# Hyena filters split into two parts where they are made, stored in both parts, and loaded so for the sums over n1

## The chip, the cores and the metric

The kernel runs on one core of one Trainium2 chip. The metric is the device time of one execution in microseconds. TensorE's clock has two levels, 2.4 and 1.2 GHz; the profile prints the granted clock as a share of the higher one.

## The reference, cut to what matters

One encoder block on x of 2048 x 1024, float32: a projection, differential attention, a Hyena mixer, a merge, and a mixture of 16 experts. The part that matters here is the Hyena mixer with its implicit filters:

```
filt = (hid @ w_out).reshape(l, HYENA_ORDER, 2, HYENA_WIDTH)      # hid: 2048 x 64
filt = filt * exp(-t[:, None] * deltas[None, :])[:, None, None, :]
kern = concatenate([filt[:, :, 0], zeros(1, ...), filt[:0:-1, :, 1]])
spec = rfft(kern, axis=0)
...
hy = short_conv(u @ w_in[hyena columns])       # width 3; z, g1, g2 of 512 channels each
for n in range(2):
    z = gates[n] * (long_conv(z, spec[:, n]) + skip[n] * z)
```

So there are 2 orders x 2 sides x 512 channels of filters of 2048 taps, and each is brought into the frequency domain once.

## The kernel before

float32 products are made on TensorE from two parts: a number a is written as a high part (a rounded copy, type F32R) and a low part (a minus the high part), and `mm3` does three matmuls, high x high, low x high and high x low. `split` makes the parts with a copy on ScalarE and a subtraction on VectorE, `split_pool` with the subtraction on POOL instead.

Every engine takes its instructions in order. The order is set when the program is built: a list scheduler goes through the instructions as written and places each by its own estimate of when it can start; pools with a fixed number of buffers make it wait for the last reader of a buffer. DMAs are issued by SP (`nc.sync`), ScalarE (`nc.scalar`) and POOL (`nc.gpsimd`), each in its own order.

**Making the filters** (`filter_gen`, called from `proj_phase` as `gen`, 309 to 600 us). The projection of the Hyena columns goes through column blocks 3, 4 and 5 of 512 columns (`weights(3 + c)`), each of 8 row blocks: a load "r" of 256 KB on SP (four buffers) and its split into "wh" and "wl" (nine buffers each). A column block has 4 x 4 groups of 24 matmuls (tile "p", operands "uh", "ul" and "wh", "wl"). Beside it, `filter_gen` is a generator whose 64 pieces are spread over the first 46 of these 48 groups. It goes through 4 channel tiles (ct), 2 orders (o), 4 stretches of 512 taps (i) and 2 combinations of the two sides (s). For each ct and o it loads and splits a factor ("wo", "weo", "woh", "wol"); for each i it loads the decay ("dc", SP) and the hidden rows ("hs", POOL); for each s two matmuls write "fq", VectorE multiplies it by the decay into "fo" (ring of two), and `store_l1` stores "fo" in two DMAs on SP of 128 KB, in rows of 512 bytes.

**Using them** (`hyena_phase`, 1510 to 2100 us). The length is split in two factors, and the transform is a sum over n1 (`first`), a middle transform (`spectrum` or `conv`) and, for the way back, a sum over the second factor (`last`, which loads "vr" on SP, splits it into "vh" and "vl", and whose matmuls are "p<-vh,d"). There are 12 `first`s: 8 of filters, 4 of the signal. Each takes 8 tiles of four channels from the generator `parts_of`: a load "zr" of 256 KB on SP (ring of three), then `split_pool` into "zh" (ScalarE) and "zl" (POOL). For each tile there are 4 x 3 matmuls of 256 columns ("p<-d,zh" and "p<-d,zl"), and the result is split into "bh" (ScalarE) and "bl" (VectorE), two of each a tile. The tails of the convolution before (tables "tg" on POOL, "yl" on POOL, "vo" on ScalarE, stored as s_v on ScalarE's queue) and `last` run beside a `first`, as does the making of the gates (loads "gu" on POOL) beside the first two.

Of the kernel before, what the change touches and what calls it, by code (L numbers as in the profile page):

```python
# [9 lines left out]
F32 = mybir.dt.float32  # L10
F32R = mybir.dt.float32r
# [8 lines left out]
L = 2048  # L20
# [73 lines left out]
def proj_phase(E, x, norm1_g, w_in, conv_w, conv_b, qg, kg, rope, qn, kn, vs, hyc, ud, sg, mlp, gen):  # L94
# [6 lines left out]
    with ExitStack() as ctx:  # L101
# [76 lines left out]
        with pool_of(tc, name="pj_q", bufs=2) as pq:  # L178
            with pool_of(tc, name="pj_x", bufs=4) as px, pool_of(tc, name="pj_pt", bufs=3, space=PSUM) as pt:
                turn(0, px, pt)  # L180
                w = weights(0)
                gq = pc.tile([128, 2, DK], F32, name="gq")
                nc.sync.dma_start(gq[:, 0], dap(qg, 0, [[0, 128], [1, DK]]))
                nc.sync.dma_start(gq[:, 1], dap(kg, 0, [[0, 128], [1, DK]]))
                rp = pc.tile([128, NT, 2, 16], F32, name="rp")
# [443 lines left out]
def filter_gen(E, w, tabs, hsd, filt):  # L629

    nc, tc = E.nc, E.tc
    with pool_of(tc, name="fl_o", bufs=2, side="right") as po, pool_of(tc, name="fg_ps", bufs=2, space=PSUM) as ps:
        for ct in range(4):
            for o in range(2):
                wo = po.tile([128, 2, 128], F32, name="wo", bufs=1)
                for s in range(2):
                    nc.sync.dma_start(wo[s * 64:(s + 1) * 64], w["w_out"][0].rearrange("h (o s c) -> h o s c", o=2, s=2)
                                      [:, o, :, ct * 128:(ct + 1) * 128])
                weo = po.tile([128, 2, 128], F32, name="weo", bufs=1)
                nc.vector.tensor_tensor(weo[:, 0], wo[:, 0], wo[:, 1], ALU.add)  # L640
                nc.vector.tensor_tensor(weo[:, 1], wo[:, 0], wo[:, 1], ALU.subtract)
                wh = po.tile([128, 2, 128], F32R, name="woh")
                wl = po.tile([128, 2, 128], F32R, name="wol")
                split(nc, wh, wl, weo)
                for i in range(4):
                    dc = po.tile([128, 512], F32, name="dc")
                    nc.sync.dma_start(dc, tabs["decay"][ct * 128:(ct + 1) * 128, i * 512:(i + 1) * 512])
                    hs = po.tile([128, 512], F32R, name="hs")
                    nc.gpsimd.dma_start(hs, hsd[:, i * 512:(i + 1) * 512])
                    fs = []  # L650
                    for s in range(2):
                        p = ps.tile([128, 512], F32, name="fq")
                        for a, ww in enumerate((wh, wl)):
                            nc.tensor.matmul(p, ww[:, s], hs, start=a == 0, stop=a == 1)
# [5 lines left out]
                    if i == 0:  # L660
                        c = po.tile([128, 1], F32, name="c0")
                        nc.vector.tensor_tensor(c, fs[0][:, 0:1], fs[1][:, 0:1], ALU.add)
                        nc.vector.tensor_scalar(fs[0][:, 0:1], c, 0.5, None, ALU.mult)
                    for s in range(2):
                        store_l1(nc.sync, filt, (o * 2 + s) * CW * L, ct, i, fs[s])
                    yield


def hyena_phase(E, hyc, filt, skip, tabs, scr, hT, filler, then):
# [7 lines left out]
    with pool_of(tc, name="hy_d", bufs=1) as pd, ExitStack() as right:  # L677
        with ExitStack() as ctx:
# [21 lines left out]
            with pool_of(tc, name="hy_e", bufs=1) as pe:  # L700
                ex = pe.tile([8, 128], F32, name="ex")
                nc.sync.dma_start(ex, tabs["ex"])
                sk = pe.tile([8, 2, 64], F32, name="sk")
                for o in range(2):
                    nc.sync.dma_start(sk[:, o], dap(skip, o * CW, [[64, 8], [1, 64]]))
                skb = pd.tile([128, 2, 64], F32, name="skb")
                p = s1.tile([128, 128], F32, name="p1")
                nc.tensor.matmul(p, ex, sk.rearrange("p o g -> p (o g)"), start=True, stop=True)
                nc.scalar.activation(skb, p.rearrange("p (o g) -> p o g", o=2), AF.Copy)
# [13 lines left out]
            def parts_of(jobs):  # L723

                todo = [(src, hf * 8 + q) for src, hf in jobs for q in range(8)]
                loads, ready = [], []

                def load():
                    src, q = todo.pop(0)
                    r = p1.tile([128, 4, 128], F32, name="zr", bufs=AHEAD)  # L730
                    nc.sync.dma_start(r, dap(src, q * 512, [[8192, 128], [128, 4], [1, 128]]))
                    loads.append(r)

                def cut():
                    r = loads.pop(0)
                    zh = p1.tile([128, 4, 128], F32R, name="zh", bufs=CUT[0])
                    zl = p1.tile([128, 4, 128], F32R, name="zl", bufs=CUT[0])
                    split_pool(zh, zl, r)
                    ready.append((zh, zl))
                    if todo:  # L740
                        load()
# [3 lines left out]
                cut()  # L745
                while ready:
                    while loads and len(ready) < CUT[0]:
                        cut()
                    yield ready.pop(0)

            AHEAD, CUT = 3, [2]

            def first(it, v, side, busy=False):
# [3 lines left out]
                for q in range(8):  # L757
                    zh, zl = next(it)
# [980 lines left out]
```

## Time and profile before

| | us |
|---|---|
| median of 3 runs (3725.71 to 3728.37) | 3728.32 |
| the profiled execution | 3731.11 |
| its span | 3729.3 |
| making the filters beside the projection | 309 to 600 |
| attention | 690 to 1510 |
| the twelve sums over n1, with all between | 1533 to 2035 |

The profile is of one execution; its engines' times are read against its own span. A window gives the busy time of each engine in a stretch, and TensorE's granted clock. A timeline gives each instruction's start, and the idle time ahead of it with what ended it. A tile's answer gives the durations of all instructions that read or write it, and of its DMAs the time from issue to landing.

### The profile page before, as it was taken

What the parts mean: (1) busy time and instruction counts of PE and PEld (TensorE: products, weight loads), DVE (VectorE), ACT (ScalarE), POOL (GpSimd) and SP (SyncE); (2) the same over time, 40 slices, a digit from 0 to 9 for tenths busy, and PEclk for the clock granted to TensorE, in tenths of its full rate; (3) what the DMA queues carried; (4) which work ended last, traced back from release to release, by engine and by line L of the source; (5) the groups of instructions that cost most, each with busy time, mean ns of one, the idle gap of its engine ahead of it and who ended that gap; (6) DMA issues with size and microseconds to landing.
All of it is one profiled execution on the core that took longest, in us unless ns stands there. A gap on an engine that the chain in (4) does not pass through costs nothing. (4 is left out here: it accounts for less than half of the span.)

```text
span 3729.3 us, 55700 instructions
## 1 busy us (share of the span) xinstructions
PE 3608.1 (97%) x21122; PEld 3117.1 (84%) x21122; DVE 2472.5 (66%) x5459; ACT 1819.2 (49%) x2787; POOL 412.9 (11%) x423
## 2 busy tenths in 40 slices
PE   8999999999999999999999799998999999999998
PEld 6788888788888888788998678887998888888887
DVE  8944552598989898256787754548875666665663
ACT  5411111566676666357667533323445555555553
POOL 0000000000000000344553200000000101101000
PEclk9999999999999999999999899998999999999999
DMA  4286774322222231757776853324666766766664
GB/s 157 75 246 170 193 187 135 119 64 68 96 81 94 68 102 60 227 165 227 210 214 192 286 170 130 115 91 138 216 194 204 222 206 208 221 203 210 220 204 123
DMA packets 449713, 607.28 MB, mean 163 GB/s; under 512 B 37467, under 2 KB 333411, under 8 KB 442789
## 3 DMA queue, kind: packets, MB, share of 16 engines
q1 hardware_dynamic: 388149, 436.71, 37.1%
q0 software_dynamic: 34736, 127.16, 12.7%
q10 hardware_dynamic: 26560, 39.85, 3.0%
q8 instruction: 166, 2.72, 0.3%
q14 instruction: 102, 0.84, 0.1%
HBM read 464.16 MB, written 139.46 MB: 162 GB/s over the span
## 5 line engine op out<-in xcount | busy, mean ns | idle before, releaser
L43 DVE TENSOR_TENSOR wl<-r,wh 128x2048 fp32r<-128x2048 f32 (+1 forms) x248 | 476.9, 1928 | 333.1 <-ACT wh L42 333.0
L42 ACT ACTIVATE wh<-r 128x2048 fp32r<-128x2048 f32 (+1 forms) x248 | 402.5, 1624 | 383.6 <-PE pg L1616 138.4
L1616 PE MATMUL pg<-x,wh 128*128 128x512 f32 x1664 | 587.0, 398 | 0.0
L1619 PE MATMUL pg<-x,wl 128*128 128x256 f32 x1664 | 466.3, 280 | 0.0
L1616 PEld LDWEIGHTS pg<-x,wh 128*128 128x128 f32 x1664 | 312.4, 188 | 75.3
L411 DVE TENSOR_SCALAR_CACHE_REDUCE x<-p 128x512 f32<-128x512 f32 x512 | 335.0, 685 | 22.8 <-PE p L410 22.0
L410 PE MATMUL p<-k,qT 128*128 128x512 f32 x1024 | 327.3, 415 | 0.0
L1619 PEld LDWEIGHTS pg<-x,wl 128*128 128x128 f32 x1664 | 314.1, 189 | 0.5
L418 ACT ACTIVATE x<-x,sm 128x2048 f32<-128x2048 f32 x128 | 256.7, 2005 | 45.8 <-DVE sm L415 42.0
L42 ACT ACTIVATE ah<-pt 128x512 fp32r<-128x512 f32 x256 | 150.2, 595 | 151.9 <-PE pt L433 151.3
L48 PE MATMUL p<-wh,uh 128*128 128x512 f32 x512 | 203.5, 398 | 0.4 <-ACT uh L134 0.4
L49 PE MATMUL py<-wl,hh 128*128 128x512 f32 x512 | 203.3, 397 | 0.0
L48 PE MATMUL py<-wh,hh 128*128 128x512 f32 x512 | 201.8, 394 | 0.0
L43 DVE TENSOR_TENSOR bl<-p,bh 128x512 fp32r<-128x512 f32 x192 | 124.6, 685 | 115.5 <-ACT bh L42 114.7
L49 PE MATMUL p<-wl,uh 128*128 128x512 f32 x512 | 200.5, 392 | 0.4 <-DVE wl L43 0.4
L50 PE MATMUL py<-wh,hl 128*128 128x512 f32 x512 | 200.5, 392 | 0.0
L43 DVE TENSOR_TENSOR al<-pt,ah 128x512 fp32r<-128x512 f32 x256 | 174.9, 686 | 38.5 <-ACT ah L42 37.5
L50 PE MATMUL p<-wh,ul 128*128 128x512 f32 x512 | 200.4, 392 | 0.0
L410 PEld LDWEIGHTS p<-k,qT 128*128 128x128 f32 x1024 | 171.3, 189 | 24.4 <-ACT qT L368 2.8
L433 PE MATMUL pt<-idf,x 128*128 128x128 f32 x1024 | 164.7, 272 | 0.0
L48 PE MATMUL gp<-gh,gu 128*128 128x512 f32 x384 | 158.3, 412 | 4.1 <-ACT go L294 3.4
L1642 POOL DMA_INDIRECT out_dram<-y,ix x32 | 67.8, 2118 | 808.0 <-ACT y L1641 698.3
(433 smaller groups left out, 9346.8 us busy)
## 6 DMA issues: line engine op xcount, KB each, us to landing
r<-in_w_gate SPq DMA_DIRECT2D x64, 1024.0 KB, 5.2
r<-in_w_up SPq DMA_DIRECT2D x64, 1024.0 KB, 5.8
r<-in_w_down SPq DMA_DIRECT2D x64, 1024.0 KB, 5.8
gu<-s_ud POOLq DMA_DIRECT2D x48, 1024.0 KB, 5.9
tg<-in_tg POOLq DMA_DIRECT2D x68, 384.0 KB, 4.2
xt<-in_x SPq DMA_DIRECT2D x32, 512.0 KB, 4.3
s_filt<-fo SPq DMA_DIRECT2D x128, 128.0 KB, 3.2
zr<-s_filt SPq DMA_DIRECT2D x64, 256.0 KB, 3.1
```

The lines of the kernel that those rows point to most:

```text
L42: nc.scalar.activation(hi, src, AF.Copy)
L43: return nc.vector.tensor_tensor(lo, src, hi.bitcast(F32), ALU.subtract)
L48: nc.tensor.matmul(out, a[0], b[0], start=start, stop=False)
L49: nc.tensor.matmul(out, a[0], b[1], start=False, stop=False)
L50: return nc.tensor.matmul(out, a[1], b[0], start=False, stop=stop)
L410: nc.tensor.matmul(p, qT[:, t * 2 + m, a], k2[:, m, o:o + 512], start=a == 0, stop=a == 1)
L411: nc.vector.tensor_scalar(x[:, o:o + 512], p, 0.125, None, ALU.mult, ALU.max, accum_out=sm[:, c * 2 + i:c * 2 + i + 1])
L418: nc.scalar.activation(x, x, AF.Exp, bias=sm[:, 8 + m:9 + m], accum_out=acc)
L433: nc.tensor.transpose(p[:, i, t * 128:(t + 1) * 128], EX[u, t, 0][:, (g * 2 + i) * 128:(g * 2 + i + 1) * 128], E.idf)
L1616: nc.tensor.matmul(p.rearrange("p a c -> p (a c)"), wt[0][:, k, cs], x2[:, k].rearrange("p a c -> p (a c)"), start=k == 0, stop=False, ski ...
L1619: nc.tensor.matmul(p[:, 0], wt[1][:, k, cs], x2[:, k, 0], start=False, stop=k == KD - 1, skip_group_check=True)
L1642: nc.gpsimd.indirect_dma_start(out=rows, out_offset=bass.IndirectOffsetOnAxis(ap=ix[:, s:s + 1], axis=0), in_=y, in_offset=None, compute_o ...
```

## The change

In `filter_gen` the factors of both orders are made at the start of a channel tile (in buffers of the ring "dc"), and the order o becomes the inner loop of the stretch i, so that decay and hidden rows are loaded once for both orders. A new function `keep` splits a filter tile in place ("fo" is now 128x4x2x128, F32R, 512 KB, still two buffers) and stores it in two DMAs of 256 KB on SP, high and low part side by side in rows of 1 KB. The scratch for the filters doubles. In `parts_of`, the tiles of filters (64 of 96) are loaded by POOL, 512 KB each with both parts, straight into operands "zz" (ring of four); the tiles of the signal are still loaded by SP, into the buffers "ya" and "vo", and split by ScalarE and POOL into "zz". The small tables "gq" and "rp" move to a pool that lives shorter.

```diff
+        def keep(f, o, s, ct, i):
+            raw = f[:, :, 1].bitcast(F32)
+            split(nc, f[:, :, 0], f[:, :, 1], raw)
+            for h in range(2):
+                nc.sync.dma_start(dap(filt, (o * 2 + s) * CW * L * 2 + ((ct * 2 + h) * 16 + i * 4) * 16384,
+                                      [[256, 64], [16384, 4], [1, 256]]),
+                                  f[h * 64:(h + 1) * 64].rearrange("p a b c -> p a (b c)").bitcast(F32))
...
-                    dc = po.tile([128, 512], F32, name="dc")
...
+            ww = [factors(ct, o) for o in range(2)]
+            for i in range(4):
+                dc = po.tile([128, 4, 128], F32, name="dc")
...
+                for o in range(2):
...
-                        f = po.tile([128, 512], F32, name="fo")
-                        nc.vector.tensor_tensor(f, p, dc, ALU.mult)
+                        f = po.tile([128, 4, 2, 128], F32R, name="fo")
+                        nc.vector.tensor_tensor(f[:, :, 1].bitcast(F32), p.rearrange("p (a b) -> p a b", b=128), dc,
+                                                ALU.mult)
                         fs.append(f)
                         if s == 0:
+                            if i:
+                                keep(f, o, s, ct, i)
                             yield
...
-                    for s in range(2):
-                        store_l1(nc.sync, filt, (o * 2 + s) * CW * L, ct, i, fs[s])
+                        keep(fs[0], o, 0, ct, i)
+                    keep(fs[1], o, 1, ct, i)
                     yield
...
-                    r = p1.tile([128, 4, 128], F32, name="zr", bufs=AHEAD)
-                    nc.sync.dma_start(r, dap(src, q * 512, [[8192, 128], [128, 4], [1, 128]]))
-                    loads.append(r)
+                    src, q, two = todo.pop(0)
+                    z = p1.tile([128, 4, 2, 128], F32R, name="zz", bufs=AHEAD)
+                    r = None
+                    if two:
+                        nc.gpsimd.dma_start(z.rearrange("p a b c -> p (a b c)"),
+                                            dap(src, q * 1024, [[16384, 128], [1, 1024]]))
+                    else:
+                        r = px.tile([128, 4, 128], F32, name=("ya", "vo")[q % 2], bufs=2)
+                        nc.sync.dma_start(r, dap(src, q * 512, [[8192, 128], [128, 4], [1, 128]]))
+                    loads.append((z, r))
...
-                    split_pool(zh, zl, r)
+                    if r is not None:
+                        split_pool(z[:, :, 0], z[:, :, 1], r)
...
-            it = parts_of([(filt[0, 0], 0), (filt[0, 1], 0)])
+            it = parts_of([(filt[0, 0], 0, True), (filt[0, 1], 0, True)])
...
-    filt, hsd = scratch("filt", (2, 2, CW, L)), scratch("hsd", (128, L))
+    filt, hsd = scratch("filt", (2, 2, CW, L, 2)), scratch("hsd", (128, L))
```

The order of the instructions moves with it. On SP, while column block 4 ends and 5 begins, before (a row is a line, an operation, a destination and a source, a shape and how many follow each other; "s_filt" are the filter stores, two a tile, "s_hyc" those of the projection):

```order
L143 DMA r<-in_w_in 128x512 x2
L56 DMA s_filt<-fo 64x4x128 x4
L56 DMA s_hyc<-s 64x4x128 x4
L143 DMA r<-in_w_in 128x512
L647 DMA dc<-in_decay 128x512 x2
L143 DMA r<-in_w_in 128x512 x3
L56 DMA s_filt<-fo 64x4x128 x4
L647 DMA dc<-in_decay 128x512
L56 DMA s_hyc<-s 64x4x128 x2
L143 DMA r<-in_w_in 128x512 x2
```

and now:

```order
L653 DMA s_filt<-fo 64x4x256 x4
L143 DMA r<-in_w_in 128x512
L653 DMA s_filt<-fo 64x4x256 x4
L143 DMA r<-in_w_in 128x512
L653 DMA s_filt<-fo 64x4x256 x4
L143 DMA r<-in_w_in 128x512
L661 DMA dc<-in_decay 128x512
L639 DMA dc<-in_filt_w_out 64x2x128 x2
L143 DMA r<-in_w_in 128x512 x4
```

The three single "r" here are row blocks 5, 6 and 7 of column block 5, behind the stores of tiles 40, 42 and 44; before, in the piece above, the first two "r" are row blocks 5 and 6, the next one is row block 7, and the others are of the block after.

On TensorE at the same place, before (two matmuls of "fq" are one filter tile):

```order
L48 MATMUL p<-uh_147,wh 128x512
L49 MATMUL p<-ul_148,wh 128x512
L654 MATMUL fq<-hs,woh 128x512
L654 MATMUL fq<-hs,wol 128x512
L50 MATMUL p<-uh_147,wl 128x512
L48 MATMUL p<-uh_487,wh 128x512
L49 MATMUL p<-ul_488,wh 128x512
L50 MATMUL p<-uh_487,wl 128x512
```

and now:

```order
L670 MATMUL fq<-hs,woh 128x512
L670 MATMUL fq<-hs,wol 128x512
L670 MATMUL fq<-hs,woh 128x512
L670 MATMUL fq<-hs,wol 128x512
L670 MATMUL fq<-hs,woh 128x512
L670 MATMUL fq<-hs,wol 128x512
L48 MATMUL p<-uh_147,wh 128x512
L49 MATMUL p<-ul_148,wh 128x512
L48 MATMUL p<-uh_487,wh 128x512
L49 MATMUL p<-ul_488,wh 128x512
L50 MATMUL p<-uh_147,wl 128x512
L50 MATMUL p<-uh_487,wl 128x512
```

The three filter tiles are 42, 43 and 44, and the next matmuls take one row block (5) to four groups at once ("uh_147", "uh_487" and two more); before, one group went through all row blocks with one filter tile between.

On ScalarE in the sum whose window before is 1690 to 1704 us, before:

```order
L42 ACTIVATE bh<-p_16872 128x32x16
L820 DMA s_v<-vo 128x2x128
L720 ACTIVATE zh<-zr 128x512
L42 ACTIVATE bh<-p_16887 128x32x16
L42 ACTIVATE bh<-p_16896 128x32x16
L720 ACTIVATE zh<-zr 128x512
L42 ACTIVATE bh<-p_16911 128x32x16
L42 ACTIVATE bh<-p_16920 128x32x16
L720 ACTIVATE zh<-zr 128x512
L42 ACTIVATE bh<-p_16935 128x32x16
L42 ACTIVATE bh<-p_16944 128x32x16
L720 ACTIVATE zh<-zr 128x512
```

and now:

```order
L42 ACTIVATE bh<-p_16818 128x32x16
L843 DMA s_v<-vo 128x2x128
L42 ACTIVATE bh<-p_16827 128x32x16
L42 ACTIVATE bh<-p_16838 128x32x16
L42 ACTIVATE bh<-p_16847 128x32x16
L42 ACTIVATE bh<-p_16858 128x32x16
L42 ACTIVATE bh<-p_16867 128x32x16
L42 ACTIVATE bh<-p_16878 128x32x16
L42 ACTIVATE bh<-p_16887 128x32x16
L42 ACTIVATE vh<-vr 128x512
```

The "zh" between the "bh" are gone, and the last store of v stands behind the fifth "bh" of the sum, where it stood behind the sixth.

## Rows read from the trace of the kernel before

**Rows 1.** The page, part 1: busy us, share of the span, instructions of each engine.

```profile
PE 3608.1 (97%) x21122; PEld 3117.1 (84%) x21122; DVE 2472.5 (66%) x5459; ACT 1819.2 (49%) x2787; POOL 412.9 (11%) x423
```

**Rows 2.** Windows, the making (364 to 414) and three sums over n1; columns in the first line.

```profile
core 0: us, PE busy (x) PEld busy (x) DVE busy (x) ACT busy (x) POOL busy (x), PEclk, DMA share, GB/s
364.00:414.00 50.00, 50.00 (x221) 41.04 (x220) 28.17 (x52) 9.92 (x17) 3.13 (x6) 1.00 0.70 184
1533.00:1552.00 19.00, 16.45 (x109) 14.17 (x108) 8.99 (x14) 12.46 (x23) 13.37 (x15) 1.00 0.96 302
1725.00:1739.00 14.00, 12.86 (x103) 12.25 (x102) 12.40 (x21) 13.15 (x28) 8.08 (x7) 1.00 0.70 216
1823.00:1837.00 14.00, 13.46 (x109) 13.02 (x107) 9.32 (x15) 10.70 (x21) 9.67 (x10) 1.00 0.84 230
```

**Rows 3.** Tile fo; ns min/median/max, first and last start; the landing is of its stores.

```profile
L56 SPq DMA_DIRECT2D s_filt<-fo x128: 574/610/1021, 316.5 to 591.5; - x128
L656 DVE TENSOR_TENSOR fo<-fq,dc x64: 678/691/692, 315.2 to 590.1; 128x512 f32<-128x512 f32 x64
DMA to landing us min/median/max: 2.4/3.2/4.2
```

**Rows 4.** Tile r, 300 to 700 us: split of the weights, and the landing of their loads.

```profile
L43 DVE TENSOR_TENSOR wl<-r,wh x31: 680/684/693, 299.7 to 599.9; 128x512 fp32r<-128x512 f32 x31
L42 ACT ACTIVATE wh<-r x30: 631/634/637, 299.8 to 597.9; 128x512 fp32r<-128x512 f32 x30
DMA to landing us min/median/max: 2.8/3.4/7.6
```

**Rows 5.** Tile zr: the split of a loaded tile on ScalarE and POOL.

```profile
L720 ACT ACTIVATE zh<-zr x96: 615/632/681, 1532.3 to 2031.2; 128x512 fp32r<-128x512 f32 x96
L721 POOL TENSOR_TENSOR zl<-zr,zh x96: 1269/1294/1455, 1533.0 to 2031.9; 128x512 fp32r<-128x512 f32 x96
```

**Rows 6.** Tile p, 1500 to 2110 us: the split of a sum.

```profile
L43 DVE TENSOR_TENSOR bl<-p,bh x192: 673/684/693, 1537.2 to 2035.5; 128x512 fp32r<-128x512 f32 x192
```

**Rows 7.** Timeline, the gap ahead of 1706.81: start, us, engine, what [idle before, releaser].

```profile
1697.52 0.37 ACTq L820 DMA_DIRECT2D s_v<-vo  x1
...
1701.89 0.37 SPq L866 DMA_DIRECT2D vr<-s_v  x1
...
1704.80 0.63 ACT L42 ACTIVATE vh<-vr 128x512 fp32r<-128x512 f32 x1 [0.61 <-DMA vr<-s_v]
1705.34 1.07 ACT L42 ACTIVATE bh<-p 128x512 fp32r<-128x512 f32 x2
...
1706.07 2.66 DVE L43 TENSOR_TENSOR bl<-p,bh 128x512 fp32r<-128x512 f32 x4
...
1706.81 0.38 PE L48 MATMUL p<-vh,d 128*128 128x256 f32 x1 [2.31 <-DVE bl L43]
```

**Rows 8.** Timelines: a wait of TensorE in the first sum, and one in the last filter sum.

```profile
1535.68 0.39 PE L48 MATMUL p<-d,zh 128*128 128x256 f32 x1 [1.55 <-ACT zh L720]
...
1996.13 0.63 ACT L720 ACTIVATE zh<-zr 128x512 fp32r<-128x512 f32 x1 [1.27 <-DMA zr<-s_filt]
...
1999.66 0.39 PE L48 MATMUL p<-d,zh 128*128 128x256 f32 x1 [2.10 <-DVE bl L43]
```

**Rows 9.** Windows, the stretches behind two such gaps; columns as in rows 2.

```profile
1706.80:1710.80 4.00, 3.99 (x19) 3.74 (x20) 2.77 (x5) 2.14 (x5) 2.73 (x2) 0.58 0.86 255
1999.60:2004.40 4.80, 4.74 (x27) 4.74 (x28) 3.78 (x7) 3.50 (x8) 3.12 (x3) 0.64 0.92 307
```

**Rows 10.** The page, part 6: KB of one transfer and us to landing.

```profile
gu<-s_ud POOLq DMA_DIRECT2D x48, 1024.0 KB, 5.9
tg<-in_tg POOLq DMA_DIRECT2D x68, 384.0 KB, 4.2
zr<-s_filt SPq DMA_DIRECT2D x64, 256.0 KB, 3.1
```

More of the change, by code (lines that the diff above doesn't have):

```diff
@@ new lines, in factors @@
+        def factors(ct, o):
+            wo = po.tile([128, 4, 128], F32, name="dc")
+            for s in range(2):
+                nc.sync.dma_start(wo[s * 64:(s + 1) * 64, :2],
+                                  w["w_out"][0].rearrange("h (o s c) -> h o s c", o=2, s=2)
+                                  [:, o, :, ct * 128:(ct + 1) * 128])
+            nc.vector.tensor_tensor(wo[:, 2], wo[:, 0], wo[:, 1], ALU.add)
+            nc.vector.tensor_tensor(wo[:, 3], wo[:, 0], wo[:, 1], ALU.subtract)
+            wh = po.tile([128, 2, 128], F32R, name="woh")
+            wl = po.tile([128, 2, 128], F32R, name="wol")
+            split(nc, wh, wl, wo[:, 2:])
+            return wh, wl
@@ L699, in hyena_phase @@
             nc.gpsimd.dma_start(d3, tabs["d3"])
[L700 to L709, printed above, removed]
+            AHEAD = 4
+            e2 = p1.tile([8, 2, 128], F32, name="zz", bufs=AHEAD)
+            nc.sync.dma_start(e2[:, 0], tabs["ex"])
+            for o in range(2):
+                nc.sync.dma_start(e2[:, 1, o * 64:(o + 1) * 64], dap(skip, o * CW, [[64, 8], [1, 64]]))
+            skb = pd.tile([128, 2, 64], F32, name="skb")
+            p = s1.tile([128, 128], F32, name="p1")
+            nc.tensor.matmul(p, e2[:, 0], e2[:, 1], start=True, stop=True)
+            nc.scalar.activation(skb, p.rearrange("p (o g) -> p o g", o=2), AF.Copy)
             TF = {}
@@ L723, in parts_of @@
             def parts_of(jobs):
[L725 removed]
+                todo = [(src, hf * 8 + q, two) for src, hf, two in jobs for q in range(8)]
                 loads, ready = [], []
                 def load():
[L729 to L739 removed]
+                    src, q, two = todo.pop(0)
[8 more added lines that the diff above has]
+                    loads.append((z, r))
+                def cut():
+                    z, r = loads.pop(0)
+                    if r is not None:
+                        split_pool(z[:, :, 0], z[:, :, 1], r)
+                    ready.append(z)
+                while todo and len(loads) < AHEAD:
+                    load()
+                while loads:
+                    while loads and len(ready) < 3:
+                        cut()
+                    yield ready.pop(0)
                     if todo:
                         load()
[L743 to L751 removed]
+                yield from ready
             def first(it, v, side, busy=False):
@@ L757, in first @@
                 for q in range(8):
-                    zh, zl = next(it)
+                    z = next(it)
                     for a in range(2):
@@ L918, in hyena_phase @@
                 for hf in range(2):
[L919 to L920 removed]
+                    jobs += [(filt[o, 0], hf, True), (filt[o, 1], hf, True), ((hyc, z1)[o], hf, False)]
             it = parts_of(jobs[2:])
```

38 lines of the change are left out of this document (12 added, 26 removed).

## The prediction

> **What bounds the kernel now.** The first view is the page's busy times: TensorE is busy for 97% of the span [rows 1], so an edit pays only where TensorE stands idle or runs at half clock, and costs wherever it makes TensorE wait. The second is the table of windows, taken where the change acts [rows 2]. While the filters are made (364 to 414 us) TensorE has no idle time at all, VectorE is busy for 28 of 50 us and ScalarE for 10: nothing can be won there, only lost. In the sums over n1 it does idle: 2.55 us of the 19 us of the very first sum, 1.14 us of 14 in the one from 1725 us, 0.54 in the one from 1823 us. In the window from 1725 us ScalarE is busy for 13.15 of 14 us, VectorE for 12.40 and POOL for 8.08, so three engines are close together. The third is the waits behind such a sum, read instruction by instruction [rows 7, 8], with the clock of the stretches that follow [rows 9].
>
> The profiled execution took 3731.11 us for a span of 3729.3; the median of the runs is 3728.32, 2.8 lower. I sum against 3731.1 and take 2.8 off at the end.
>
> **The change, part by part. First the making.** The multiplications (0.691 us each) stay. For each of the 64 filter tiles the change adds a copy on ScalarE and a subtraction on VectorE, both of 128x512; the nearest rows are the weights' splits, 0.634 and 0.684 us [rows 4]. That is 64 x 0.63 = 41 us on ScalarE and 64 x 0.68 = 44 us on VectorE over some 275 us [rows 3]; with 10 and 28 us of 50 busy, both have room, so this work itself costs nothing: the projection's matmuls cover it. The loads of decay and hidden rows fall from 32 to 16 each, 16 issues less on SP and on POOL; nobody waited for them on TensorE, so nothing is won. The stores keep their number (128) and double in size.
>
> What does cost is the longer life of a tile in the ring "fo" of two. Before: multiplication 0.69, two issues on SP of 0.61, landing 3.2 [rows 3], 5.1 us. After: 0.69 + 0.63 + 0.68, one issue 0.61 ahead of the second store, and a landing that I take from the 256 KB weight loads, 3.4 [rows 4]: 6.0 us for two tiles in flight, 3.0 us a tile. The 62 tiles that are spread over the projection stand 4.4 us apart on average (275/62), so on average there is room. At the change of the weight block from column block 4 to 5 there isn't, in the new order: weight row block 5 is loaded behind the stores of tile 40, row block 6 behind those of 42, row block 7 behind those of 44 (the first pair of order fences), and the planner has pulled tiles 41 to 46 together on TensorE to fill the hole. I walk it by rows, from the start of the multiplication of tile 41. Tile 43 needs the buffer of 41 and starts at 6.0, tile 44 needs that of 42, which came 1.6 us later, so 7.6. It is split at 9.6, its stores are issued at 10.8, the weight load behind them takes 0.4 to issue and 3.4 to land (14.6), and the copy makes row block 7's high part at 15.2. By then TensorE has 29 projection matmuls and 6 tiles of two matmuls to do; at 50.00 us for 221 [rows 2], 0.226 each, that is 41 x 0.226 = 9.3 us. **It waits about 6 us**, in two or three pieces. The other two changes of weight block (3 to 4, and to the gate's) have 39 and some 70 matmuls, 9 and 16 us, between the last tile ahead of a weight load and its first use, and the same walk from that tile gives 8 to 11 us: nothing there, or little. The lower bound is 0: before, two tiles' stores also stood ahead of row block 7, and no window shows idle time. The upper is 15: the landing at its longest (4.2, [rows 3]) in both rounds, 3 us more at each of the other changes of block, and a stretch at half clock behind the wait, for which [rows 9] give 1.7 us.
>
> **Second, the sums over n1 of the filters, 8 of the 12.** ScalarE loses 64 copies of 0.632 us (40 us) and POOL 64 subtractions of 1.294 (83 us) [rows 5]. In a sum that is 5.1 of ScalarE's 13.15 us and all of the filter's work on POOL. What is late next is VectorE: 16 subtractions of 0.684 [rows 6] are 10.9 us, and with the previous convolution's tail it had 12.40 of the 14. TensorE's own work is 12.86. So not all of the idle time can go: with 2.55 us in the first sum and a mean of 0.84 in seven others (the two shown), 8.4 us in all, I take half, **4 us**. Between 0 and 8.4.
>
> Against it stand the loads. 256 KB on SP become 512 KB on the POOL queue, in a ring of four. A load goes out when TensorE has left the tile four back, so three tiles cover it: 36 matmuls of 256 columns at 12.86/103 us [rows 2] are 4.5 us. No load of 512 KB on that queue is in the trace; 384 KB take 4.2 us from issue to landing and 1024 KB 5.9 [rows 10], so 4.5 to 4.6 between them. Cover and load are equal; with the fourth tile only once in a sum, I put 0.3 us, times 8, **2 us**. The lower bound is 0. The upper is 12: 1.5 us a sum, if the landing goes to the 5.9 of the larger tile, for the filter's bytes alone double and this stretch already has a DMA share of 0.70 to 0.96 [rows 2].
>
> The Trainium skill (DMA: Bandwidth & Descriptors, Anatomy of one DMA — SWDGE (gpsimd) path) fits a transfer of this queue as 2.0 us plus its bytes at 436 GB/s, an estimate of 3.2 us here. The same fit gives 2.9 us for the 384 KB that took 4.2, so the trace disagrees. By it the 2 us would not arise.
>
> **Third, the gaps behind a sum.** Three times TensorE stands for about 2.3 us ahead of the first sum over the second factor ("p<-vh,d"); the one at 1706.81 is shown [rows 7]. The chain: the last store of v goes out at 1697.52, the load "vr" behind it at 1701.89, the copy "vh" starts at 1704.80, the two "bh" behind it on ScalarE at 1705.34, "bl" at 1706.07, TensorE at 1706.81: 9.3 us from store to use. TensorE ran out 2.3 us earlier. Most of this chain is transfers, which the change doesn't touch. In the new order of ScalarE the store stands one half tile earlier (after the fifth "bh" and not the sixth; 0.75 us of TensorE's work) and no "zh" stands between. So the gap shrinks by 0.75, three times, 2.3 us. Behind each gap comes a stretch at half clock, 4.00 us at a granted 0.58 [rows 9], worth 1.7 us; whether a gap of 1.6 us still brings one no row says (the 1.55 us ahead of 1535.68 did not [rows 8, 2]), so I put 0.4 of 3 x 1.7, 2.0 us. Together **4 us**, between 0 and 12 (gaps and stretches gone).
>
> **Fourth, the wait at 1999.66**: 2.10 us [rows 8] and again 1.7 at half clock [rows 9], where ScalarE had stood 1.27 us for a late "zr" of the filter. I take half, **2 us**; 0 to 3.8.
>
> **The sum.** 3731.1 + 6 (weight block) - 4 (sums) + 2 (loads) - 4 (gaps) - 2 (late load) = 3729.1, less 2.8: **3726 us**. Copies, subtractions, fewer loads and the move of two small tables to another pool count zero. A difference under 0.2%, 7.5 us, is about what a measurement of this kernel can't tell from none; my sum is inside it.
>
> **The rivals.** *All the gaps go.* Without the split ScalarE and POOL are never behind, both transfers land while TensorE works, and the three gaps, the late load and their half clock go (12 + 3.8), with 4 us from the sums, and the wait at the weight block is only 4. With the loads covered that is 3731.1 - 15.8 - 4 + 4 - 2.8 = 3712 us. For it: ScalarE is the busiest of the helpers in the sum from 1725 us. Against: the chain in [rows 7] is mostly the store and the load of v. Chance 0.31.
>
> *TensorE starves at the weight block.* This one ends slower. SP's queue is in order, and each weight load waits behind a store that waits for VectorE, which waits for a landing. If the walk above meets its upper end, 15 us and not 6, it eats all of the gain, and with the gaps as they were (4 us less won) the time is 3726 + 9 + 4 = 3739. It decides from some 12 us of waiting, with the gaps unchanged. For it: the new orders of SP and TensorE put the tiles there in a heap. Against: TensorE met no idle time there with a chain of 5.1 us. Chance 0.17.
>
> *The POOL queue is late.* The 64 loads leave SP for POOL's queue, behind gate and table loads that wait for TensorE. If each sum waits 1.5 us for its fifth tile, 12 us instead of 2, the sum is 3736. For it: DMA share up to 0.96 in the first sum. Against: 384 KB on the same queue land in 4.2 us in the middle of this stretch. The Trainium skill (SBUF — State Buffer, SBUF: two separate sides) speaks for this rival: a transfer issued from GpSimd may stand still while VectorE holds the port that both share. The landing of 4.2 us [rows 10], beside a VectorE at 12.40 of 14 us, shows no such stop. Chance 0.10.
>
> **How the numbers follow.** My forecast, within 0.2%, has 0.42; the first rival 0.31 (faster by over 0.2%); the other two 0.27 (slower by over 0.2%). The range reaches to the cases on both sides, 3711 to 3740: its lower end is the first rival's time, its upper end the starved weight block with the gaps unchanged.
>
> **What would show it.** In the window of the making, idle TensorE in one place of 4 to 8 us around the change from column block 4 to 5, ended by "wh" or by "fo": if there is none, the walk is wrong. In the sums, "zz" as the releaser of TensorE for tenths of a microsecond once in a sum; whole microseconds would be the third case. Ahead of "p<-vh,d", gaps of about 1.6 us and half clock behind some of them; three gaps of 2.3 would say that v's transfers alone set them. ScalarE must lose 40 us in the sums and gain as much in the making, POOL lose 83. A total outside 3711 to 3740 means that a wait I have not seen was made or removed.

## The result, and the profile after

The changed kernel takes 3770.27 us (median, 3766.72 to 3778.26); the kernel before took 3728.37 beside it (3725.71 to 3732.94). The ratio is 1.0107 [1.0096, 1.0119]: **42 us slower**, where 3726 us was predicted and 3740 was the upper end. Of the profiled executions (3731.11 and 3778.26 us) the spans are 3729.3 and 3776.5. Cut at the first or last matmul of a kind on TensorE, they divide like this:

| stretch (us) | before | after |
|---|---|---|
| making: first "fq" to the gate's first "gp" | 373.3 | 394.1 |
| attention: first to last "p<-k,qT" | 782.4 | 789.9 |
| the twelve sums: first "p<-d" to first "pb" | 561.8 | 581.1 |
| all else | 2011.8 | 2011.4 |

The difference is 20.8 + 7.5 + 19.3 - 0.4 = 47.2 us, two about equal losses and a smaller one in attention, which the change doesn't touch. The profiled execution of after is the slowest of its five, 8 us above the median.

The page of after, part 1 (beside [rows 1]):

```profile
PE 3625.1 (96%) x21122; PEld 3126.8 (83%) x21122; DVE 2517.8 (67%) x5523; ACT 1826.5 (48%) x2787; POOL 356.1 (9%) x407
```

TensorE has the same 21122 matmuls, but 17.0 us more of busy time: some run at half clock. Windows of the making, columns as in [rows 2]:

```profile
364.00:414.00 50.00, 50.00 (x221) 40.97 (x220) 30.16 (x58) 12.82 (x23) 1.31 (x2) 1.00 0.69 180
...
500.00:514.00 14.00, 11.52 (x51) 8.82 (x49) 6.14 (x9) 2.53 (x4) 0.53 (x1) 0.99 0.68 174
514.00:540.00 26.00, 19.45 (x56) 13.47 (x57) 13.47 (x24) 8.22 (x15) 1.06 (x2) 0.74 0.80 223
540.00:564.00 24.00, 24.00 (x107) 19.77 (x106) 16.35 (x33) 5.13 (x9) 0.53 (x1) 1.00 0.84 224
```

The damage is where the prediction looked for it, at the change from column block 4 to 5: 2.48 us idle in the second row and 6.55 in the third, which also ran at a granted 0.74. The kernel before was full there:

```profile
514.00:564.00 50.00, 50.00 (x221) 41.14 (x220) 24.40 (x47) 5.23 (x9) 3.17 (x6) 1.00 0.69 175
```

It runs 221 matmuls in 50 us, 0.226 us each. After runs 56 from 514 to 540 us, 12.7 us of work at full clock, so 13.3 of these 26 us are lost: 6.55 idle, and 6.8 in slower matmuls. The granted clock stood at its lower level, 1.2 GHz, from 513.9 to 524.1 us and from 534.4 to 537.7. The first and last rows are full, as before. The timeline of that place (start, us, engine, what, idle before and releaser):

```profile
509.00 4.82 SPq L653 DMA_DIRECT2D s_filt<-fo  x4
...
510.42 0.69 DVE L672 TENSOR_TENSOR fo<-fq,dc 128x512 f32<-128x512 f32 x1 [1.45 <-DMA s_filt<-fo]
...
513.23 0.69 DVE L672 TENSOR_TENSOR fo<-fq,dc 128x512 f32<-128x512 f32 x1 [0.67 <-DMA s_filt<-fo]
...
513.97 0.79 PE L670 MATMUL fq<-hs,woh 128*128 128x512 f32 x1 [2.07 <-DVE fo L672]
...
515.38 4.92 SPq L653 DMA_DIRECT2D s_filt<-fo  x4
516.92 0.69 DVE L672 TENSOR_TENSOR fo<-fq,dc 128x512 f32<-128x512 f32 x1 [1.56 <-DMA s_filt<-fo]
...
517.66 0.80 PE L670 MATMUL fq<-hs,woh 128*128 128x512 f32 x1 [2.47 <-DVE fo L672]
...
519.96 0.69 DVE L672 TENSOR_TENSOR fo<-fq,dc 128x512 f32<-128x512 f32 x1 [0.31 <-DMA s_filt<-fo]
...
522.11 5.48 SPq L653 DMA_DIRECT2D s_filt<-fo  x4
...
524.19 0.69 DVE L672 TENSOR_TENSOR fo<-fq,dc 128x512 f32<-128x512 f32 x1 [2.11 <-DMA s_filt<-fo]
...
527.63 0.80 SPq L143 DMA_DIRECT2D r<-in_w_in  x1
...
531.91 0.63 ACT L42 ACTIVATE wh<-r 128x512 fp32r<-128x512 f32 x1 [5.80 <-DMA r<-in_w_in]
...
532.60 0.50 PE L48 MATMUL p<-uh,wh 128*128 128x512 f32 x1 [3.40 <-ACT wh L42]
```

The "fo" rows of VectorE are tiles 40 to 44, each ended by a landing of stores: 6.73 us from tile 41 to 43, 7.27 from 42 to 44. SP is held for about 5 us by each four stores, and the load of row block 7 (527.63) goes out when the last of them is issued. At the gate's block there is one more wait, 2.16 us at 633.10, for "wh" too; from 600 to 640 us TensorE runs 159 matmuls where it ran 178, some 4 us lost. With the 13.3 and the 2.5 of the second row this is 20 of the 20.8 us, 11.3 of them idle time and the rest slower matmuls.

In the sums, tile zz: who waited for it (us, times) and its loads' landing (min/median/max):

```profile
  PE p L48: 17.8, 10
...
DMA to landing us min/median/max: 3.8/5.9/11.0
```

TensorE waits ten times for a load, 17.8 us in all. The windows of the whole stretch, before and after, and one of the sum that rows 2 show from 1823 us:

```profile
1533.30:2095.10 561.80, 523.66 (x3966) 498.48 (x3964) 372.78 (x680) 357.39 (x721) 257.39 (x251) 0.99 0.70 208
1560.10:2141.20 581.10, 533.47 (x3969) 507.92 (x3969) 374.75 (x680) 327.58 (x658) 207.56 (x250) 0.96 0.76 230
1868.00:1882.00 14.00, 10.40 (x74) 9.76 (x72) 6.53 (x10) 5.86 (x11) 3.26 (x7) 0.90 1.07 358
```

TensorE is idle for 38.1 us before and 47.6 after: other waits went while those for "zz" came. Its busy time with the same matmuls grows by 9.8 us, at a granted clock of 0.96 and not 0.99, so half of the 19.3 us is slower work. In the last row the DMA engines are full and move 358 GB/s, where they moved 230 before [rows 2]; TensorE stands idle for 3.6 of 14 us, where it stood for 0.54. (A transfer counts in the window in which it starts, so a share can pass 1.)

The longest wait, a timeline at the end of the second sum:

```profile
1635.61 1.06 POOL L855 DMA_DIRECT2D tg<-in_tg  x2 [4.60 <-PE p L50]
...
1636.66 0.55 POOL L753 DMA_DIRECT2D zz<-s_filt  x1
...
1637.17 0.56 POOL L855 DMA_DIRECT2D tg<-in_tg  x1
...
1646.21 0.55 PE L48 MATMUL p<-d,zz 128*128 128x256 f32 x1 [7.51 <-DMA zz<-s_filt]
```

and the window around it (columns as in [rows 2]):

```profile
1632.00:1645.00 13.00, 6.71 (x53) 6.33 (x51) 5.38 (x8) 6.08 (x12) 2.12 (x4) 0.95 0.94 299
```

The load was issued at 1636.66, behind two tables and 2.3 us after TensorE had left its buffer (1634.39), and came at 1646.08, 9.4 us after its issue. DMA engines were busy for 0.94 of the window and moved 299 GB/s, where TensorE had 6.71 of 13 us of work: here the transfers bound the kernel, not an engine. They are mostly not the filter's: of the 12 DMAs issued in this window one is a filter load.

### The profile page after: what moved, and what is told of

The parts are those of the page before. It is cut to its first block, busy times and chain, and to the rows that moved or that the text cites. A ratio compares the mean times of both kernels' runs of the same rounds, so it can differ in the third digit from the quotient of the medians.

```text
span 3776.5 us, 55615 instructions
## 1 busy us (share of the span) xinstructions
PE 3625.1 (96%) x21122; PEld 3126.8 (83%) x21122; DVE 2517.8 (67%) x5523; ACT 1826.5 (48%) x2787; POOL 356.1 (9%) x407
## 5 line engine op out<-in xcount | busy, mean ns | idle before, releaser
L42 ACT ACTIVATE wh<-r 128x2048 fp32r<-128x2048 f32 (+1 forms) x248 | 402.3, 1624 | 386.6 <-PE pg L1638 138.5
L48 PE MATMUL p<-uh,wh 128*128 128x512 f32 x384 | 151.5, 395 | 3.9 <-ACT wh L42 3.9
```

The source lines that it names most:

```text
L42: nc.scalar.activation(hi, src, AF.Copy)
L48: nc.tensor.matmul(out, a[0], b[0], start=start, stop=False)
```

## The experiments

All in one table: the ratio to the kernel before with its interval, and of the profiled executions the stretches that the table above calls making and sums.

| kernel | us | ratio | making | sums |
|---|---|---|---|---|
| after | 3770.27 | 1.0107 [1.0096, 1.0119] | 394.1 | 581.1 |
| e1 making alone | 3746.95 | 1.0046 [1.0027, 1.0064] | 394.1 | 563.4 |
| e2 sums alone | 3750.18 | 1.0053 [1.0036, 1.0071] | 373.6 | 581.8 |
| e7 loop order alone | 3727.24 | 0.9986 [0.9977, 0.9996] | 373.3 | 557.7 |
| e11 split, half of it stored | 3728.92 | 1.0002 [0.9992, 1.0012] | 376.3 | 560.3 |
| e8 order outer again | 3790.67 | 1.0169 [1.0147, 1.0191] | 412.7 | 577.1 |
| e3 stores on POOL | 3775.24 | 1.0115 [1.0091, 1.0140] | 391.8 | 582.8 |
| e14 stores on ScalarE | 3771.44 | 1.0106 [1.0089, 1.0122] | 390.8 | 587.7 |
| e15 stores on SP and POOL | 3770.72 | 1.0102 [1.0085, 1.0118] | 396.4 | 583.2 |
| e6 three "fo" | 3782.22 | 1.0147 [1.0125, 1.0169] | 400.4 | 588.3 |
| e9 three "fo", other room | 3794.84 | 1.0174 [1.0157, 1.0191] | 412.8 | 584.3 |
| e12 stores on POOL, three "fo" | 3765.93 | 1.0095 [1.0078, 1.0112] | 390.5 | 576.3 |
| e13 the same room, two "fo" | 3781.39 | 1.0134 [1.0116, 1.0152] | 403.0 | 580.6 |
| e16 weight loads on ScalarE | 3769.05 | 1.0092 [1.0070, 1.0115] | 386.6 | 582.3 |
| e17 the same, three "fo" | 3764.35 | 1.0092 [1.0070, 1.0115] | 382.7 | 580.3 |
| e4 filter loads on SP | 3763.64 | 1.0087 [1.0064, 1.0110] | 392.7 | 573.3 |
| e5 half the bytes | 3753.48 | 1.0064 [1.0043, 1.0084] | 392.3 | 565.2 |
| e10 half the bytes, on SP | 3748.70 | 1.0051 [1.0034, 1.0068] | 391.7 | 557.5 |

**Which half of the change (e1, e2).** e1 keeps the new making and has the sums of the kernel before, which load 256 KB on SP and split it (both parts of two channels of the doubled scratch, so other numbers):

```diff
-                        nc.gpsimd.dma_start(z.rearrange("p a b c -> p (a b c)"),
-                                            dap(src, q * 1024, [[16384, 128], [1, 1024]]))
+                        nc.sync.dma_start(r, dap(src, q * 1024, [[16384, 128], [128, 4], [1, 128]]))
...
+                    split_pool(zh, zl, r)
```

> The making as in the changed kernel (split and stored in both parts, order as the inner loop); the sums over n1 as before: 256 KB loads on SP from the doubled scratch and the split on ScalarE and POOL. The loads take both parts of two channels instead of one value of four, so the filters' values are not those of the reference; the work and the bytes are. Theory (the cost of the changed kernel has two places, some 19 us in the making and some 20 us in the sums): 3747 us, with 11 us of idle TensorE and 5 at half clock around the change from column block 4 to 5. Rival (the making only moves idle time that the next stage gives back): 3728 to 3732 us.

e2 has the old making and the new sums, whose 512 KB loads read the undoubled scratch (they reach over the next channels, so other numbers):

```diff
-                                            dap(src, q * 1024, [[16384, 128], [1, 1024]]))
+                                            dap(src, min(q, 14) * 512, [[8192, 128], [1, 1024]]))
```

> The sums as in the changed kernel (512 KB loads on POOL into ring of four, no split of filters), the making as before. The 512 KB rows reach over the next channels of the undoubled scratch, so the values are not those of the reference. Theory (late loads): 3728 + 20 = 3748 us, with TensorE waiting for zz in most filter sums. Rival (the sums were disturbed only by what the making left, such as another order of the gate's work): 3728 us or a few less, since ScalarE and POOL lose their splits.

Both came as their theories said: 17 and 20 us, 37 of the 40 that the ratio of after stands for. Within the intervals the two halves add up. In attention, e7 took 789.6 us, as long as after, and is not slower as a whole; the others with the same attention took 780.6 to 789.2. So the 7.5 us there are not shown to belong to the change; what makes attention scatter is open.

**The parts of the making (e7, e11, e8).** e7 is the kernel before with the order as inner loop, and nothing else:

```diff
+            W = []
...
-                for i in range(4):
+                W.append((wh, wl))
+            for i in range(4):
...
+                for o in range(2):
...
-                        for a, ww in enumerate((wh, wl)):
+                        for a, ww in enumerate(W[o]):
```

> The kernel before with the order as the inner loop of the making and nothing else: decay and hidden rows loaded once for both orders, tiles and stores of 256 KB as before. Theory (the loop's order is free): 3728 us within 5, no idle TensorE in the making. Rival (the exchange itself makes the planner's heap): 3735 to 3745 us.

e11 splits each tile as after does, but stores the high part alone (128 KB a store), and has the sums of before. In the making it differs from e1 in the stores, and in the order that the scheduler makes with them:

```diff
...
-                                      [[256, 64], [16384, 4], [1, 256]]),
-                                  f[h * 64:(h + 1) * 64].rearrange("p a b c -> p a (b c)").bitcast(F32))
+                                      [[128, 64], [8192, 4], [1, 128]]),
+                                  f[h * 64:(h + 1) * 64, :, 0].bitcast(F32))
```

> The making as in the changed kernel, split included, but only the high part is stored, in 128 KB DMAs of 512-byte rows as before, and the sums are as before; the values are not those of the reference. Theory (the doubled stores make the making's loss: by their landing, and by the heap that the planner makes because of them; the order it makes here is the even one): 3730 to 3735 us. Rival (the split's copy and subtraction in the ring of two make it): 3747 us as in e1.

Neither shows a loss in its total: loop and split cost nothing there, as predicted. The making of e7 is as long as before, that of e11 3 us longer, where e1 has 21. Tile fo of e11 (VectorE's idle time until stores had landed, and their landing):

```profile
  DMA s_filt<-fo: 11.4, 8
...
DMA to landing us min/median/max: 2.4/2.5/5.6
```

In after these are 25.4 us in 22 places and 3.1/3.7/4.9. So the doubled stores are what costs, with what the scheduler makes of them. e8 sets the loops back in the changed kernel:

```diff
-            ww = [factors(ct, o) for o in range(2)]
-            for i in range(4):
+            for o, i in ((o, i) for o in range(2) for i in range(4)):
+                if i == 0:
+                    ww = {o: factors(ct, o)}
...
-                for o in range(2):
+                for _ in range(1):
```

> The changed kernel with the order as the outer loop again (32 loads each of decay and hidden rows), split tiles and doubled stores kept. Theory (the split tile's life makes the loss): the loss stays, 3765 to 3780 us, in an even larger heap (eight tiles in a row at the change of block). Rival (the exchange of the loops): 3753 us.

The rival is refuted, and the loss grew beyond the theory's range: in its timeline TensorE waits 7.93 us at 510.79, 5.21 at 518.40 and 7.32 at 527.79.

**Another queue for the stores (e3, e14, e15).** If the weights only wait behind stores on SP, moving the stores should help.

```diff
-                nc.sync.dma_start(dap(filt, (o * 2 + s) * CW * L * 2 + ((ct * 2 + h) * 16 + i * 4) * 16384,
+                nc.gpsimd.dma_start(dap(filt, (o * 2 + s) * CW * L * 2 + ((ct * 2 + h) * 16 + i * 4) * 16384,
```

> The changed kernel with the filter stores issued by POOL and not by SP, so that no weight load stands behind a filter store; the ring of two stays. Theory (weight loads behind stores on SP's queue): the 16 us around the change of block go, and some 3 at the gate's block: 3770 - 17 = 3753 us. Rival (the longer life of a tile in the ring of two, 6 us instead of 5, sets it whatever queue stores): 3770 us, with TensorE waiting for fo as before.

e14 has `nc.scalar` there and e15 `(nc.sync, nc.gpsimd)[h]`.

> The changed kernel with the filter stores issued by ScalarE, ring of two. An issue there took 0.37 us (s_v) and not 0.61, and no weight load stands behind a store, so a tile's stay falls from 6.5 to some 6.2 us; the planner spreads the tiles 17 to 20 matmuls apart. Theory (stay and queue together): the loss in the making falls to 0 to 6 us, 3770 - 13 = 3757 us. Rival (ScalarE, in order, then holds the projection's copies behind each split): 3770 us.

> The changed kernel with one half of each filter store issued by SP and the other by POOL, ring of two; the planner's order is the even one of e11. The two issues run side by side, so a tile's stay falls by 0.6 us to some 6 us. Theory (stay): the loss falls to 3 to 8 us, 3770 - 11 = 3759 us. Rival (any weight load behind a store is enough): 3768 to 3775 us.

All three theories missed: the making stays at 391 to 396, where five kernels with the making of after (after, e1, e4, e5, e10) have 391.7 to 394.1. In e3 the scheduler's order is as even as before, the heap of tiles is gone, and VectorE waits for landings all the same, 38.6 us in 28 places (e14: 60.7, e15: 72.8); e11 has an even order and half the bytes, and loses 3 us. So the order of the heap is not the cost by itself.

**A third buffer (e6, e9, e12, e13).** There is no free room for it; e6 takes a weight buffer (8 for 9), e9 one of "hs" and one of the projection's output.

```diff
-                        f = po.tile([128, 4, 2, 128], F32R, name="fo")
+                        f = po.tile([128, 4, 2, 128], F32R, name="fo", bufs=3)
```

> The changed kernel with three buffers for the filter tiles fo in the making instead of two; the room is taken from the weights' ring, eight buffers instead of nine. Theory (the ring of two, with a tile in use for 6.5 us, sets the making's loss): 3 tiles in 6.5 us instead of 2, the wait around the change of block falls from 16 us to under 5, 3770 - 11 = 3759 us. Rival (SP's order alone, weight loads behind stores): 3770 us; and if the ninth weight buffer matters, more.

> The changed kernel with three buffers for the filter tiles fo, as in e6_ring3, but the room taken from the hidden rows (one buffer instead of two) and the projection's output tiles s (two instead of three); the weights keep nine buffers. Theory (the ring of two sets the making's loss, and e6 paid for the missing weight buffer): 16 us of waits in the making fall under 6, 3770 - 10 = 3760 us. Rival (weight loads behind stores on SP, whatever the ring): 3770 us, waits for wh at the changes of block.

Both missed, and both got slower. e6, timeline:

```profile
515.19 9.24 SPq L653 DMA_DIRECT2D s_filt<-fo  x8
...
527.28 2.05 SPq L143 DMA_DIRECT2D r<-in_w_in  x4
...
531.02 0.79 PE L48 MATMUL p<-uh,wh 128*128 128x512 f32 x1 [8.49 <-ACT wh L42]
```

The waits for "fo" shrink to 5.1 us in 4 places, and with one tile more in flight eight stores stand in a row on SP ahead of the weight loads: the same wait, one buffer further on. Why e9, with other room, loses most (412.8) is not taken apart. e12 takes the stores off SP as well, with room from the weights' loads (three "r") and the output; e13 is its control, the same without the third buffer.

> The changed kernel with the filter stores on POOL (as e3_stores_pool) and three buffers for fo; the room comes from the raw weights (three buffers instead of four) and the output tiles s (two instead of three). Theory (a tile's stay in the ring of two, 7 us on POOL against 4.4 us a tile, sets the loss once the queue is out of the way): the 18 us of e3's making fall under 5, 3775 - 14 = 3760 us. Rival (bytes in flight, not buffers): 3775 us.

> The same as e12 with two buffers for fo: the control for the room taken from the raw weights and the output tiles. Theory: as e3, 3775 us or a few more. If it is as fast as e12, the third buffer does nothing.

The third buffer is worth 15 us (12.5 of them in the making), but the room costs 7 us first (e13 against e3; 11 in the making), so the net gain is small; e12 lies between its theory and its rival. In e12 VectorE's waits for stores are 6.1 us, yet TensorE waits 5.76 us at 416.26 for "wh": the weight loads now stand on SP behind stores of the projection.

**Another queue for the weights (e16, e17).**

```diff
-                E.last_load = nc.sync.dma_start(r, w_in[0, k * 128:(k + 1) * 128, c * 512:(c + 1) * 512])
+                E.last_load = (nc.scalar if c > 3 else nc.sync).dma_start(r, w_in[0, k * 128:(k + 1) * 128, c * 512:(c + 1) * 512])
```

> After, with the weight loads of column blocks 4, 5 and the gate's on ScalarE's queue and the filter stores left on SP: the first kernel of the study in which stores and weight loads have different queues while the stores stay where they were. From the first filter matmul to the gate's first matmul the changed kernel takes 394.1 us, the kernel before 373.3. If the stores at the head of SP's queue are what holds the weights back, the filter tiles no longer heap at the change from block 4 to 5, TensorE's waits there (2.07, 2.47 and 3.40 us) go, the making falls to about 384 and the time to about 3760. The rival, by the runs that moved the stores: the waits for wh become waits for fo at other places, the making stays at 391 to 394 and the time at 3768 to 3775.

> The same, with a third buffer for fo (and 8 buffers for the weights in place of 9, for room). With the ring of three alone the waits for fo were gone, but eight stores in a row stood ahead of a weight load on SP (8.49 us of waiting at 531.02). If fo's two buffers and SP's order are the whole cost, the making comes within 5 us of the kernel before (378) and the time is 3753 to 3757, the sums' 20 us being left. If it is the doubled bytes themselves, weight loads landing late beside them whatever the queue, or the room, the making stays above 388 and the time above 3765.

The making falls to 386.6 and, with the third buffer, to 382.7: 7.5 and 11.4 us of 20.8. e17, the window that was at the heart of the loss:

```profile
500.00:514.00 14.00, 12.13 (x49) 8.56 (x48) 10.51 (x18) 5.49 (x10) 0.53 (x1) 1.00 0.96 287
514.00:540.00 26.00, 26.00 (x115) 21.40 (x115) 12.88 (x24) 5.71 (x10) 0.53 (x1) 1.00 0.79 207
```

The second row is full and at full clock. So neither expectation holds whole: SP's order and the two buffers together are about half of the loss. The queue alone wins 7.5 us, the third buffer alone (e6) loses 6, and on top of the queue it wins 4 more. The other half, 9.4 us, is not taken apart, and its cause stays open: what is seen of it is smaller waits (1.87 us idle in the first row, beside a DMA share of 0.96), and e17 pays for its room with a weight buffer. In the total times the gain is 6 us by the ratio of either kernel (1.0092 against 1.0107), less than the intervals, which reach 8 us to either side.

**The sums (e4, e5, e10).** e4 issues the 512 KB on SP, e5 loads one half and uses its two channels twice (256 KB, other numbers), e10 is both.

```diff
-                        nc.gpsimd.dma_start(z.rearrange("p a b c -> p (a b c)"),
-                                            dap(src, q * 1024, [[16384, 128], [1, 1024]]))
+                        nc.gpsimd.dma_start(z.rearrange("p a b c -> p (a b c)")[:, :512],
+                                            dap(src, q * 1024, [[16384, 128], [1, 512]]))
```

> The changed kernel with the 64 filter loads of 512 KB issued by SP and not by POOL; bytes, ring and tiles as in the changed kernel. Theory A (bytes: the sums ask more than the transfers give): the landings stay at 6 to 7 us inside a sum and the time within 5 us of 3770. Theory B (the queue: a load stands behind tables and gate loads that wait for TensorE): the waits for zz go, 3770 - 15 = 3755 us.

> The changed kernel with each filter load of the sums halved: 256 KB (both parts of two channels, used twice) on POOL, same ring of four, same matmuls; the values are not those of the reference. Theory (bytes: 512 KB a tile land too late): most of the 20 us in the sums go, 3750 us, with landings of some 4 us and hardly a wait for zz. Rival (POOL's order, a load behind tables and gate loads): the waits stay, 3765 to 3770 us.

> As e5_half_bytes (filter loads of 256 KB, values not those of the reference), issued by SP and not by POOL. Theory (two causes in the sums: bytes, and POOL's order, which still made 6.6 us of wait for a late zz in the second sum of e5): 3753 - 6 = 3747 us, which leaves only the making's 17 us. Rival (one cause, the bytes): 3753 us.

| sums, us | 512 KB | 256 KB |
|---|---|---|
| on POOL | 582.2 (mean of 12 kernels, 576.3 to 588.3) | 565.2 |
| on SP | 573.3 | 557.5 |
| as before, with split | | 560.8 (mean of 4, 557.7 to 563.4) |

e5 and e10 came near their theories (3750 and 3747), e4 between its two. The bytes are worth 16 to 17 us in either row, POOL's queue 8 to 9 in either column; the scatter is 3 to 6. By total times the bytes are 13 to 16 us (e10 against e4, e5 against after); the queue is 5 to 8, within the intervals. Waits of TensorE's first matmuls for zz fall with them: 17.8 us (after), 12.2 (e4), 10.2 (e5), 8.2 (e10). Landings: 5.9 median (after), 5.7 (e4), 3.9 (e5), 3.8 (e10); of the loads on SP only 25 and 21 of 64 have a landing in the trace. So SP isn't seen to make a transfer faster. The longest wait tells of POOL's order: at the same tile, the last of the second sum, TensorE waits 7.51 us in after and 6.64 in e5, where the load goes out 2.3 us after its buffer came free, and 2.54 in e4 and 2.03 in e10, where it goes out at once. These 5 us are more than half of what the queue costs; for the rest its order is likely, and not shown. The Trainium skill (SBUF — State Buffer, SBUF: two separate sides) says that transfers issued from GpSimd can stand still while an instruction of VectorE in a two-port mode holds the port that both share; 5.9 against 5.7 us shows no such stop here.

**The best version** of all is e7, 0.9986 [0.9977, 0.9996]: the loop exchange alone, with half the loads of decay and hidden rows. No stretch of its profile shows where the 5 us come from.

## Why the prediction was wrong

**The making: mechanism right, size wrong.** Place, chain and releasers ("fo", then "wh") are the predicted ones; 6 us became 17 to 21. The failing step is the start of the walk. It began at tile 41 with a ring in which the next tile could follow 1.6 us later, and with all 41 matmuls of TensorE still to do. But tiles 39 and 40 already stood in the ring: tile 42 waits for the buffer of 40 and starts 3.69 us after tile 41 (516.92 against 513.23), and by 513.23 TensorE had done 9 of the 41. A stay was 6.7 and 7.3 us and not 6.0, and from tile 44 to the high part of row block 7 it took 8.4 and not 7.6. So the high part is made 19.3 us after the start (531.91 + 0.63 - 513.23), not 15.2, and 32 matmuls, 7.2 us, stand against it, not 9.3: 12.1 us and not 6. Of these 6 us more, 4 are the start of the walk, 1.3 the stay and 0.8 the last piece.

The other 8 of the 20 us lie around the walk: 1.7 of waits ahead of its start (of the 2.48 before 514), 2 of half clock behind the wait, for which the upper bound had 1.7, and 4 at the gate's block, which was put at "nothing there, or little". The half clock from 513.9 to 524.1 us adds nothing to these: it only fills part of the wait for row block 7, whose chain goes through landings, VectorE, SP and ScalarE.

**The sums: the loads mis-sized.** 2 us with an upper bound of 12; it was about 16 for the bytes and 8 for POOL's queue. The failing step is the landing of 4.5 to 4.6 us, taken from 384 KB at 4.2 and 1024 KB at 5.9 [rows 10]. Those were medians in the old traffic, and the change doubled the filter's part of it. 3.8 us is the fastest of the 64 loads; the median is 5.9 and the slowest 11.0, against 4.5 of cover. A balance of bytes would have shown it: 8 tiles of 256 KB more in the 14 us of a sum [rows 2] are 150 GB/s on top of 216 to 230, some 370 to 380, though four tiles can come ahead; the fullest row there moved 302 at a share of 0.96, and after moved 358 at its fullest here. The share of 0.70 to 0.96 stood in [rows 2], and was used for the upper bound alone. The walk also had no term for half clock behind these waits, and slower matmuls are half of the sums' 19.3 us. The Trainium skill (DMA: Bandwidth & Descriptors, Anatomy of one DMA — SWDGE (gpsimd) path) has a fit that gives an estimate of 3.2 us for such a load; the trace disagrees, even at its fastest, 3.8.

**The gains.** 4 us from the sums' idle time: e10, where bytes and queue are as before, has sums of 557.5 against 560.8, 3 us and within the scatter; it may be there, and it isn't shown. 4 us from the gaps ahead of "p<-vh,d": wrong. After:

```profile
1743.33 0.39 PE L48 MATMUL p<-vh,d 128*128 128x256 f32 x1 [2.01 <-DVE bl L43]
```

The other two are 0.91 at 1882.85 and 3.90 at 2017.73, together 6.8 us where three of 2.3 [rows 7] were 6.9. All three end when ScalarE gets "vr": the transfers of v set them, as the case against the first rival said, and in the last one the load "vr" took from 2012.68 to 2017.05 among the larger loads. The late "zr" at 1999.66 [rows 8] became late "zz": 1.15 us at 2007.26 and 1.07 at 2009.99.

**The work itself** came as told: VectorE's busy time grows by 45 us, ScalarE's by 7 (41 more, 40 less were told). POOL loses 57 us and not 83, because the page counts DMA issues on POOL as busy time: the 64 new ones of 0.53 us are 34 more, the 16 loads of hidden rows that went some 8 less.

**The rivals.** Both slower ones came, "TensorE starves" at 3739 and "the POOL queue is late" at 3736, each for about half of the loss and each larger than told (20.8 us for 15, some 19 for 12). They were given chances as if only one of them could come, but they lie in different stretches and don't exclude each other. Both at their upper bounds without the gains would have been 3731.1 + 15 + 12 - 2.8 = 3755, still 15 us short.

## What to carry to other kernels

Trading arithmetic for bytes lost here because the DMA engines had no room. Before such a trade, sum the bytes of the new transfers over the stretch in which they must come, and set that against what the DMA engines move there at a full share, before any single landing time is read. When a tile lives longer in a short ring, begin the walk where the ring is last known to be free, not at the tile in question, and follow what else stands behind its stores on the same queue. Losses in separate stretches add: they are terms of the sum, not rivals.

## What the runs showed of the hardware

- One 512 KB load on POOL's queue took 3.8 to 11.0 us to land, 9.4 at a DMA share of 0.94; issued on SP, 3.9 to 11.0 (25 of 64 on record).
- Around waits of 2.07 and 2.47 us of TensorE (ended at 513.97 and 517.66) the granted clock was at 1.2 GHz from 513.9 to 524.1 us, though it worked between them, and 0.74 in the mean from 514 to 540; slower matmuls took as much more time in that window as it was idle (6.8 beside 6.55 us).
- In the sums, 9.5 us more of idle time went with 9.8 us more of busy time for the same matmuls.
- One sum with doubled filter loads had a full DMA share and moved 358 GB/s over 14 us, where 230 had gone before.
- Attention, the same instructions in all kernels, took from 780.6 to 789.9 us.
